# Layer 1 of a two-layer encoder: v's two parts in one stationary, 384-wide weights split in pairs, last kept units in dead buffers

## The chip, the cores and the metric

The kernel runs on one core of a Trainium2 chip. The metric is the device time of one launch in microseconds (us); the time shown for a kernel is the median of its runs. Engines are named as in the profile: PE (TensorE matmuls), PEld (its weight loads), DVE (VectorE), ACT (ScalarE), POOL (GpSimd), SP (SyncE, here only a DMA queue). Each engine runs its own instructions in the order in which they were written to it; between engines there are semaphores.

## The reference

Two layers over x of 256 tokens by 1024 channels, all in float32. Each layer is a mixer and a channel sublayer:

```python
h = rms_norm(x, n1); proj = h @ w_in_l              # 1024 -> 2560
# 4 neighbourhood heads (a), 6 dilated heads (d), 6 grouped-query heads (c) on 2 key/value heads
out_a = neighbourhood_attention(...)                # softmax(q k^T * scale + bias) v
out_d = dilated_window_attention(...)
out_c = gqa_block_attention(...)
mix = concat([rms_norm(out_a, og_a), rms_norm(out_d, og_d), rms_norm(out_c, og_c)])
x = x + mix @ w_out_l
h = rms_norm(x, n2); g, u = split(h @ w_gate_up)    # 2 x 2816
x = x + (gelu(depthwise_conv(g)) * u) @ w_dn
```

Head size is 64, so two heads make 128 columns of the mixer's output.

## The kernel before

**Two parts.** Every float32 operand of a large product is split into a high part in TensorE's rounded float32 and a low part, the rest: `hi = round(z)` by ACT (a CAST in the profile, or an ACTIVATE with a scale) and `lo = z - hi` by DVE. A product is then three matmuls, hi·hi + hi·lo + lo·hi (`mm3`). Weights go by units of at most 2048 columns: `load` starts the DMA of a unit into one of four `raw` buffers from SP's queue, `split` makes its `wp_hi` and `wp_lo` (two buffers of each), in chunks: whole rows of 512 or 1024 columns, and single rows of 384 for the 384-wide projections (in a unit of four rows, four chunks).

**Kept units.** The six w_out units of layer 1 are split ahead, while layer 0's channel sublayer runs (`keep`), and stored to DRAM. In layer 1 `split` fetches them back with two DMAs each from POOL's queue into the same `wp_hi` and `wp_lo` buffers. They are, in the order of use, two for the dilated heads, two for the grouped-query heads (both 3 x 512 columns), two for the neighbourhood heads (2 x 512).

**Attention.** For each head: scores into a PSUM bank, softmax (`softens`: DVE adds the bias and finds the maximum, ACT takes exp with its sum, DVE the reciprocal, ACT scales), four transposes on PE (`turn`), the transposed probabilities split into `pT` hi (`act_ch`, ACT) and lo (`act_cl`, DVE), and the product with v (`weigh`). v is the stationary operand: 64 columns of the head beside 64 columns of zeros (`beside_zeros`), so that an even head fills rows 0 to 63 of the output bank `op` and an odd head adds rows 64 to 127. Three matmuls for each half of the keys, 256 columns each: six a head, twelve a pair. When a pair of heads is done, `mixed` scales the bank with the output norm's gain into `mixT_hi` (ACT) and `mixT_lo` (DVE) and squares it (`sqm`, ACT; POOL adds the squares of a group). After a group's last pair `group_rstd` turns the squares on PE, DVE sums them and POOL makes the root; then the group's out-projection is added to x with that root (`const_x<-psa_a`, DVE).

**End of the mixer.** The out-projections of the dilated and grouped-query groups and the later projections are PE's filler between the steps of attention. When the last group's root is there, x is complete by halves, x is transposed (`const_ident,const_x`) and made into `hT`, and the first gate product of the channel sublayer starts.

**What sets the order.** The program is recorded as a list of operations; a planner with fixed costs then gives every engine its order and every tile its slot. `PLACES` shifts single operations in rank before that. Nearly all instructions bear one helper's line in the profile, so groups are told apart by their tiles: `psa_a` and `psw_w` are the PSUM banks (four each), `act_s2k` are five working buffers of 512 columns that softmax uses, `const_v` the value tiles.

Of the kernel before, what the change touches and what calls it, by code (L numbers as in the profile page):

```python
# [23 lines left out]
HD = 64  # L24
# [14 lines left out]
NS2K = 5  # L39

# [184 lines left out]
def handover(a, b):  # L225
# [292 lines left out]
def encoder_kernel(  # L518
# [70 lines left out]
    with nc.later(1000):  # L589
# [8 lines left out]
        [const.tile([P, NT, 2 * n + 1, HD], F32R, tag=f"v{n}{i}", name=f"v{n}{i}") for i in range(2)]  # L598
# [45 lines left out]
    def load(i):  # L644
        v = views[i]
        if i in kept:
            raws.append(None)
            return
        a, b = v.shape[1], v.shape[2]
# [20 lines left out]
    def split(i):  # L670
# [3 lines left out]
        raw = raws[i]  # L674
        hi = wp.tile([P, UNIT], F32R, tag="hi", name=f"hi{i}", bufs=PARTS)
        lo = wp.tile([P, UNIT], F32R, tag="lo", name=f"lo{i}", bufs=PARTS)
        h = b if i < 2 else b * max(1, CHUNK // b)
# [201 lines left out]
    for l in range(DEPTH):  # L879
# [171 lines left out]
        def values_of(tiles, ps, c0, t, nh):  # L1051
            src = ps[:, c0 : c0 + nh * HD].rearrange("p (h d) -> p h d", d=HD)
            values([z[:, t, 1 : 2 * nh : 2] for z in tiles], src, t)

        def beside_zeros(tiles, h, odd):

            i = 2 * h + 1 - odd
            return [z[:, :, i : i + 2].rearrange("p t m d -> p t (m d)") for z in tiles]


        class Head:
# [49 lines left out]
            def weigh(self, op, first, last):  # L1111

                hi, lo = self.pT
                for kt in range(NT):
# [5 lines left out]
        def mixed(op, gi, i):  # L1120
# [4 lines left out]
            h = mixT_hi[:, k]  # L1125
            nc.scalar.activation(h, op, AF.Copy, scale=g)
# [124 lines left out]
        def weigh(i):  # L1251
            gi, h = groups[i]
            if h % 2 == 0:
                hold["op"] = psw.tile([P, S], F32, tag="w", name=f"o_{l}{i}")
# [287 lines left out]
```

## Time and profile before

| | us |
|---|---|
| median of three runs | 610.36 (610.24 to 610.68) |
| profiled execution, its own time | 611.12 |
| its span, first to last instruction | 609.3 |
| layer 0: mixer, channel sublayer | 0 to 118, 118 to 295 |
| layer 1: mixer, channel sublayer | about 304 to 420, 420 to 605 |

The boundaries of the stages are read from the windows and the timeline of PE. A row of the timeline gives the start, the length, the engine, the output tile and the operands, and in brackets the idle time before it with what ended it. Matmuls overlap in the pipeline, so what one costs on PE is the distance between two starts, not its length.

### The profile page before, as it was taken

To read this page: it belongs to the slowest core of one execution; us is meant where nothing else is said; L and a number is where in the kernel's file an instruction comes from. 1 tells how busy PE (TensorE), PEld (TensorE's weight loads), DVE (VectorE), ACT (ScalarE), POOL (GpSimd) and SP (SyncE) were. 2 spreads that over 40 slices of the span, in tenths; PEclk is the share of its full clock that TensorE was granted. 3 is DMA by queue.
4 is the path that set the end of the run, shared out by engine and by line. 5 is a ranking of instruction groups with operands and counts; after the bars stand their busy time and mean duration, and the time that the engine had idled before them with its cause. 6 is when DMAs were issued, how large, how long until landed. Compare 5 with 4: busy or idle time off the path is not lost.

```text
span 609.3 us, 9892 instructions
## 1 busy us (share of the span) xinstructions
PE 600.6 (99%) x3496; PEld 525.2 (86%) x3496; DVE 484.9 (80%) x989; ACT 428.4 (70%) x1065; POOL 84.6 (14%) x136
## 2 busy tenths in 40 slices
PE   8999999999999999999999999999999999999997
PEld 6999898888888888888899989887888888888886
DVE  4899987998779886978788898758977777777775
ACT  6889999686657666766598898757765556665661
POOL 2733130202400000000032214232000000000000
PEclk9999999999999999999999999999999999999999
DMA  8994223656598996999445626554666556556501
GB/s 272 296 294 143 62 79 107 208 175 240 185 219 288 318 338 220 373 311 305 142 142 189 224 70 242 184 199 139 208 207 200 169 185 208 173 176 204 198 10 69
DMA packets 85217, 121.44 MB, mean 199 GB/s; under 512 B 9880, under 2 KB 69880, under 8 KB 85168
## 3 DMA queue, kind: packets, MB, share of 16 engines
q1 hardware_dynamic: 82896, 112.17, 56.8%
q0 software_dynamic: 1728, 8.39, 4.0%
q8 instruction: 27, 0.44, 0.3%
q10 hardware_dynamic: 544, 0.26, 0.2%
q14 instruction: 22, 0.18, 0.1%
HBM read 110.93 MB, written 9.88 MB: 198 GB/s over the span
## 4 chain that ended last, share of the span: by engine, by line
PE 91%; POOL 2%; issue 2%; DMA 2%; ACT 1%; DVE 1%; SPq 0%; DVEq 0%; POOLq 0%
PE psw_w L472 50%; PE psa_a L472 41%; DMA wp_hi<-dram_khi 1%; POOL small_rstd L472 1%; DMA wp_raw<-in_w_in_dram 1%; ACT act_s2k L472 1%; POOL small_ms L472 0%; DVE const_x L472 0%; ACT act_hT L472 0%; POOL act_sck L472 0%; POOL act_scq L472 0%; ACT wp_hi L472 0%; SPq L472 0%; POOL const_gq L472 0%; POOL act_sqm L472 0%
## 5 line engine op out<-in xcount | busy, mean ns | idle before, releaser
L472 DVE TENSOR_TENSOR wp_lo<-wp_raw,wp_hi 128x512 fp32r<-128x512 f32 (+2 forms) x332 | 232.3, 734 | 55.1 <-ACT wp_hi L472 34.9
L472 ACT CAST wp_hi<-wp_raw 128x512 fp32r<-128x512 f32 (+2 forms) x332 | 202.4, 663 | 25.1 <-PE psw_w L472 9.9
L472 PE MATMUL psw_w<-act_hT,wp_hi 128*128 128x512 f32 x704 | 180.7, 393 | 0.0
L472 PEld LDWEIGHTS psw_w<-act_hT,wp_hi 128*128 128x128 f32 x704 | 127.8, 189 | 24.2
L472 PE MATMUL psa_a<-wp_hi,act_hT 128*128 128x384 f32 (+2 forms) x448 | 113.3, 333 | 2.0 <-ACT act_hT L472 1.3
L472 PEld LDWEIGHTS psw_w<-act_hT,wp_lo 128*128 128x128 f32 x704 | 98.4, 190 | 7.1
L472 PE MATMUL psw_w<-act_hT,wp_lo 128*128 128x256 f32 x704 | 103.0, 282 | 0.0
L472 PEld LDWEIGHTS psa_a<-wp_hi,act_hT 128*128 128x128 f32 x448 | 77.9, 189 | 5.0 <-ACT act_hT L472 1.6
L472 ACT COPY act_s2k<-psw_w 128x256 f32<-128x256 f32 x88 | 32.4, 373 | 61.7 <-PE psw_w L472 61.4
L472 PE MATMUL psa_a<-wp_lo,act_hT 128*128 128x384 f32 (+2 forms) x224 | 74.0, 332 | 0.1
L472 PE MATMUL psa_a<-wp_hi,act_cl 128*128 128x512 f32 (+1 forms) x176 | 68.8, 393 | 0.0
L472 PE MATMUL psa_a<-wp_lo,act_ch 128*128 128x512 f32 (+1 forms) x176 | 68.7, 392 | 0.0
L472 PE MATMUL psa_a<-wp_hi,act_ch 128*128 128x512 f32 (+1 forms) x176 | 68.3, 392 | 0.0
L472 DVE TENSOR_TENSOR act_s2k<-psw_w,act_s2k 128x256 f32<-128x256 f32 x88 | 36.6, 421 | 16.2 <-ACT act_s2k L472 15.9
L472 PEld LDWEIGHTS psa_a<-wp_lo,act_hT 128*128 128x128 f32 x224 | 42.2, 188 | 2.1 <-DVE wp_lo L472 1.0
L472 PEld LDWEIGHTS psa_a<-wp_hi,act_cl 128*128 128x128 f32 x176 | 33.1, 188 | 7.4
L472 PEld LDWEIGHTS psa_a<-wp_hi,act_ch 128*128 128x128 f32 x176 | 33.2, 189 | 6.7
L472 PEld LDWEIGHTS psa_a<-wp_lo,act_ch 128*128 128x128 f32 x176 | 33.1, 188 | 6.8
L472 DVE SCALAR_TENSOR_TENSOR act_s2k<-act_s2k,act_cw,act_s2k 128x255 f32<-128x255 f32 x88 | 36.8, 477 | 1.4 <-ACT act_s2k L472 1.3
L472 ACT ACTIVATE act_s2k<-act_s2k 128x512 f32<-128x512 f32 x22 | 13.9, 632 | 29.6 <-DVE act_s2k L472 29.6
L472 ACT ACTIVATE act_s2k<-act_s2k,act_cw 128x256 f32<-128x256 f32 x44 | 24.1, 595 | 15.0 <-DVE act_s2k L472 15.0
L472 POOL TENSOR_TENSOR small_rstd<-small_ms,const_mh 128x6 f32<-128x6 f32 (+2 forms) x26 | 31.3, 1204 | 2.1
(120 smaller groups left out, 795.2 us busy)
## 6 DMA issues: line engine op xcount, KB each, us to landing
wp_raw<-in_w_gate_up_dram SPq DMA_DIRECT2D x44, 1024.0 KB, 5.2
wp_raw<-in_w_down_dram SPq DMA_DIRECT2D x22, 1024.0 KB, 4.9
wp_raw<-in_w_in_dram SPq DMA_DIRECT2D x14, 768.0 KB, 4.7
wp_raw<-in_w_in_dram SPq DMA_DIRECT2D x8, 1024.0 KB, 8.9
wp_raw<-in_w_out_dram SPq DMA_DIRECT2D x8, 768.0 KB, 10.0
dram_khi<-act_mixT_hi SPq DMA_DIRECT2D x4, 768.0 KB, 4.4
dram_klo<-act_mixT_lo SPq DMA_DIRECT2D x4, 768.0 KB, 11.2
wp_lo<-dram_klo POOLq DMA_DIRECT2D x4, 768.0 KB, 4.7
```

Source lines behind the costliest of these rows:

```text
L472: getattr(o.engine.real, o.method)(*map(real, o.args), **{k: real(v) for k, v in o.kw.items()})
```

## The change

Five edits; the first two only for layer 1 (`ONE_BANK`).

1. The value tile holds the high and the low part of a head side by side, 128 columns, in place of the head and zeros: for the own-value heads the order is hi, lo, lo, hi for a pair, for the two key/value heads hi, lo, hi. ACT writes the high parts (twice for the key/value heads), DVE the low ones, for the own-value heads in two instructions in place of one.
2. `weigh` is two matmuls for each half of the keys, [hi|lo] by `pT` hi and [hi|lo] by `pT` lo: four a head, eight a pair. Each head of a pair has its own half of the bank. The two parts now lie in different partitions and have to be added: in `mixed` ACT copies the whole bank (128 x 512) to an `act_s2k` buffer, and DVE adds the other half's partitions of the copy to the bank, once for each head (64 x 256), into a new tile `mxm`. Gain, low part and squares are then taken from `mxm` and not from the bank.
3. The 384-wide units are split in chunks of two rows (768 columns).
4. The last two kept units (2 x 512 columns, for the neighbourhood heads) are fetched into the buffers `qc` and `kc` of the grouped-query heads' q and k, and this in `load`, not in `split`; they take no `wp_hi` and `wp_lo`.
5. Another `PLACES` table, with 75 entries for 58.

```diff
+ONE_BANK = (1,)
 PLACES = {
-    539: 34, 543: 38, 665: 15, 834: 24, 881: 160, 919: 134, 926: 7, 974: -38, 1092: 342, 1180: -15, 1181: -15,
...
+    315: 312, 320: 312, 462: 45, 522: -239, 523: -239, 526: -239, 527: -239, 540: -41, 587: 150, 654: -267, 894: 42,
...
     def load(i):
         v = views[i]
+        a, b = v.shape[1], v.shape[2]
+        n = a * b
         if i in kept:
             raws.append(None)
+            if 2 * n <= UNIT:
+                zs = [act.tile([P, n], F32R, tag=f"{'qk'[i % 2]}c{j}", name=f"kept{i}{j}", bufs=1) for j in range(2)]
+                for z, d in zip(zs, kept[i]):
+                    nc.gpsimd.dma_start(z, d)
+                raws[-1] = [z.rearrange("p (a b) -> p a b", b=b) for z in zs]
             return
...
-        h = b if i < 2 else b * max(1, CHUNK // b)
+        h = b if i < 2 else b * max(2 if b == _WD else 1, CHUNK // b)
...
             def weigh(self, op, first, last):
                 hi, lo = self.pT
+                if l in ONE_BANK:
+                    for kt in range(NT):
+                        for i, z in enumerate(self.pT):
+                            nc.tensor.matmul(
+                                op[:, self.h % 2], self.v[0][:, kt], z[:, kt],
+                                start=kt == 0 and i == 0, stop=kt == NT - 1 and i == 1,
+                            )
+                    return
...
             h = mixT_hi[:, k]
+            if l in ONE_BANK:
+                whole = act.tile([P, S], F32, tag="mxm", name=f"mxm{gi}{l}{i}", bufs=2)
+                small_ = act.tile([P, NT, S], F32, tag="s2k", name=f"mxs{gi}{l}{i}", bufs=NS2K)
+                nc.scalar.copy(small_, op)
+                for e, (mine, other) in enumerate(((LOW, HIGH), (HIGH, LOW))):
+                    nc.vector.tensor_tensor(whole[mine], op[mine, e], small_[other, e], op=ALU.add)
+                op = whole
             nc.scalar.activation(h, op, AF.Copy, scale=g)
             nc.vector.scalar_tensor_tensor(mixT_lo[:, k], op, g, h.bitcast(F32), ALU.mult, ALU.subtract)
```

The order moves on all engines. Three places matter below. The first is PE at the end of attention in layer 1, from the last pair's second head on. `const_v600` is the own-value tile's high part (in the change the tile with both parts), `const_v610` its low part, `act_ch`/`act_cl` are the split probabilities, `psa_a<-wp_..,act_mixT` an out-projection of a group, `act_sqm` the squares to be turned for the last group's root. Before:

```order
L472 MATMUL psw_w0_83<-act_ch0_774,const_v600_91 128x256
L472 MATMUL psw_w0_83<-act_cl0_791,const_v600_91 128x256
L472 MATMUL psw_w0_83<-act_ch0_774,const_v610_101 128x256
L472 MATMUL psa_a2_302<-wp_lo0_149,act_mixT_hi0_856 128x512
...
L472 MATMUL psw_w2_124<-const_ident0_89,act_sqm1_967 128x128 x2
...
L472 MATMUL psa_a0_157<-wp_hi1_240,act_mixT_lo0_916 128x512
L472 MATMUL psw_w1_117<-const_ident0_89,const_x0_79 128x128 x4
L472 MATMUL psw_w0_83<-const_ident0_89,const_x0_79 128x128 x4
L472 MATMUL psa_a2_302<-wp_hi0_141,act_mixT_hi0_856 128x512
```

And in the change, where the last two units are read from `act_kc` and `act_qc`:

```order
L477 MATMUL psw_w1_117<-act_ch0_747,const_v600_91 128x256
L477 MATMUL psw_w1_117<-act_cl0_758,const_v600_91 128x256
L477 MATMUL psa_a3_326<-wp_hi0_141,act_mixT_lo0_878 128x512
...
L477 MATMUL psa_a1_175<-act_kc00_910,act_mixT_hi0_832 128x512
...
L477 MATMUL psw_w3_166<-const_ident0_89,act_sqm1_939 128x128 x2
...
L477 MATMUL psa_a3_326<-act_qc10_752,act_mixT_hi0_832 128x512
L477 MATMUL psw_w2_124<-const_ident0_89,const_x0_79 128x128
L477 MATMUL psw_w1_117<-const_ident0_89,const_x0_79 128x128
...
L477 MATMUL psa_a0_157<-act_qc00_741,act_mixT_lo0_878 128x512
L477 MATMUL psw_w3_166<-act_hT0_146,wp_hi0_141 128x512
```

Between the last `const_v` product and the first `const_x` transpose there are 21 out-projection products of 512 columns before and 29 in the change; behind the transposes there were twelve more (a whole unit), now five, split around them.

The second place is ACT at the same point: it makes the last `act_ch`, and then serves the last two pairs. Before:

```order
L472 CAST act_ch0_774<-psw_w3_166 128x512
L472 ACTIVATE act_mixT_hi0_856<-psw_w1_117,const_gains0_122 128x256
L472 ACTIVATE act_sqm1_967<-psw_w1_117 128x256
L472 ACTIVATE act_mixT_hi0_856<-psw_w0_83,const_gains0_122 128x256
L472 ACTIVATE act_sqm0_866<-psw_w0_83 128x256
```

In the change:

```order
L477 CAST act_ch0_747<-psw_w0_83 128x512
L477 COPY act_s2k3_197<-psw_w2_124 128x512
L477 ACTIVATE act_sqm1_939<-act_mxm0_3717 128x256
L477 COPY act_s2k4_223<-psw_w1_117 128x512
L477 ACTIVATE act_mixT_hi0_832<-act_mxm0_3717,const_gains0_122 128x256
L477 ACTIVATE act_mixT_hi0_832<-act_mxm1_3763,const_gains0_122 128x256
L477 ACTIVATE act_sqm0_840<-act_mxm1_3763 128x256
```

Two copies of a bank are added, and the last pair's copy stands behind the squares of the pair before it.

The third place is POOL, where it fetches the kept units: the third unit (`wp_hi_240`, `wp_lo_248`, DRAM tiles `khi`/`klo`) was next after the first group's root, and it now stands behind the four loads of the last two units. Before:

```order
L472 TENSOR_TENSOR small_rstd_460<-small_ms_454,const_mh_85 128x2 [waits Pool_49]
L472 DMA wp_lo_248<-dram_klo_2446 128x1536 [waits DMAHW5_49,DMASW0_49,PE_49]
L472 TENSOR_TENSOR act_sqm_866<-act_sqm_866,act_sqm_967 128x256 [waits Activation_49]
L472 DMA wp_hi_240<-dram_khi_2431 128x1536 [waits DMAHW3_49,DMASW1_49,PE_49]
L472 DMA wp_lo_149<-dram_klo_2618 128x1536 [waits DMAHW3_49,DMASW2_49,PE_49]
```

In the change:

```order
L477 TENSOR_TENSOR small_rstd_465<-small_ms_459,const_mh_85 128x2 [waits Pool_49]
L477 DMA act_kc_910<-dram_khi_2694 128x1024 [waits DMAHW7_49,PE_49]
L477 DMA act_kc_916<-dram_klo_2714 128x1024 [waits DMAHW1_49]
L477 DMA act_qc_741<-dram_khi_2819 128x1024 [waits DMAHW5_49]
L477 DMA act_qc_752<-dram_klo_2835 128x1024 [waits DMAHW7_49]
L477 DMA wp_hi_240<-dram_khi_2406 128x1536 [waits DMASW1_49,DMAHW3_49,DMASW0_49,PE_49]
L477 DMA wp_lo_248<-dram_klo_2421 128x1536
```

More of the change, by code (lines that the diff above doesn't have):

```diff
@@ L597, in encoder_kernel @@
     vown, vkv = (
-        [const.tile([P, NT, 2 * n + 1, HD], F32R, tag=f"v{n}{i}", name=f"v{n}{i}") for i in range(2)]
+        [const.tile([P, NT, max(2 * n + 1, 6), HD], F32R, tag=f"v{n}{i}", name=f"v{n}{i}") for i in range(2)]
         for n in (H_DIL, H_GKV)
@@ L674, in split @@
         raw = raws[i]
+        if isinstance(raw, list):
+            parts.append(raw)
+            return
         hi = wp.tile([P, UNIT], F32R, tag="hi", name=f"hi{i}", bufs=PARTS)
         lo = wp.tile([P, UNIT], F32R, tag="lo", name=f"lo{i}", bufs=PARTS)
-        h = b if i < 2 else b * max(1, CHUNK // b)
+        h = b if i < 2 else b * max(2 if b == _WD else 1, CHUNK // b)
         if i in kept:
@@ L1055, in beside_zeros @@
         def beside_zeros(tiles, h, odd):
+            if l in ONE_BANK:
+                i = 3 * h + odd if len(tiles[0].shape) and tiles is vkv else 2 * h
+                return [tiles[0][:, :, i : i + 2].rearrange("p t m d -> p t (m d)")]
             i = 2 * h + 1 - odd
```

26 lines of the change are left out of this document (24 added, 2 removed), and 12 rows, old and new, of the table PLACES.

## The prediction

> **What bounds the kernel now.** I read the page first: engine totals and the chain of waits.
>
> ```profile
> span 609.3 us, 9892 instructions
> PE 600.6 (99%) x3496; PEld 525.2 (86%) x3496; DVE 484.9 (80%) x989; ACT 428.4 (70%) x1065; POOL 84.6 (14%) x136
> PE 91%; POOL 2%; issue 2%; DMA 2%; ACT 1%; DVE 1%; SPq 0%; DVEq 0%; POOLq 0%
> ```
>
> PE is busy almost throughout and holds 91% of the chain, so work taken from PE counts nearly in full if PE does not then wait. But a busy share is a mean over stages, so the windows come next: layer 1's mixer, its channel sublayer, and two stretches of attention.
>
> ```profile
> core 0: us, PE busy (x) PEld busy (x) DVE busy (x) ACT busy (x) POOL busy (x), PEclk, DMA share, GB/s
> 295.00:420.00 125.00, 123.57 (x802) 111.36 (x801) 97.41 (x248) 98.63 (x320) 31.37 (x47) 1.00 0.51 171
> 420.00:605.00 185.00, 185.00 (x990) 159.02 (x988) 139.83 (x237) 110.95 (x203) 1.26 (x3) 1.00 0.51 168
> 350.00:370.00 20.00, 20.00 (x142) 16.98 (x140) 19.67 (x60) 18.86 (x56) 2.67 (x5) 1.00 0.33 106
> 370.00:420.00 50.00, 48.60 (x325) 42.37 (x325) 34.77 (x83) 35.07 (x102) 16.40 (x26) 1.00 0.55 191
> ```
>
> In the channel sublayer PE never waits: it starts when the mixer ends and lasts as long as before. So the change is decided in the mixer, where PE has 1.4 us of idle time and DVE and ACT are near 80% (97.41 and 98.63 of 125). From 350 to 370, softmax of the dilated heads beside the grouped-query preparation, DVE is full: 19.67 of 20; behind it 15 of its 50 us are free. The two waits of PE that its timeline shows in this mixer:
>
> ```profile
> 397.66 0.47 PE L472 MATMUL psa_a<-wp_hi,act_mixT_lo 128*128 128x512 f32 x1
> 398.39 0.50 PE L472 MATMUL psa_a<-wp_hi,act_mixT_hi 128*128 128x512 f32 x1 [0.26 <-DMA wp_hi<-dram_khi]
> 414.42 0.40 PE L472 MATMUL psa_a<-wp_hi,act_mixT_lo 128*128 128x512 f32 x1
> 415.92 1.09 PE L472 MATMUL psw_w<-const_ident,const_x 128*128 128x128 f32 x8 [1.10 <-DVE const_x L472]
> ...
> 419.18 0.40 PE L472 MATMUL psa_a<-wp_lo,act_mixT_hi 128*128 128x512 f32 x1
> 419.42 0.39 PE L472 MATMUL psa_a<-wp_hi,act_mixT_lo 128*128 128x512 f32 x1
> ```
>
> A 512-column product takes 0.232 us from start to start (the last two rows), so the first wait is 0.73 - 0.23 = 0.50 us, for the third kept unit's DMA, and the second 1.50 - 0.23 = 1.27 us, for the last additions to x.
>
> **The change part by part.** First the products with v.
>
> ```profile
> 304.00:420.00 116.00, 15.33 (x96) 13.42 (x96) 2.86 (x6) 2.91 (x6) 0.00 (x0) 1.00 0.52 173
> 408.85 0.28 PE L472 MATMUL psw_w<-act_cl,const_v 128*128 128x256 f32 x1
> 408.96 0.40 PE L472 MATMUL psw_w<-act_ch,const_v 128*128 128x256 f32 x2
> 409.20 0.28 PE L472 MATMUL psw_w<-act_cl,const_v 128*128 128x256 f32 x1
> 409.32 0.28 PE L472 MATMUL psw_w<-act_ch,const_v 128*128 128x256 f32 x1
> 409.44 0.39 PE L472 MATMUL psa_a<-wp_lo,act_mixT_hi 128*128 128x512 f32 x1
> ```
>
> The first row is the windows view of the value tiles alone: 96 products in layer 1. Two for three leaves 64. Five of them go from 408.85 to 409.44, so one costs 0.118 us. PE loses 32 x 0.118 = **3.78 us**. The same shape and width stay, so nothing suggests another pace.
>
> What it adds is the fold: for each of eight pairs a copy of a bank on ACT and two additions on DVE.
>
> ```profile
> L472 ACT CAST act_ch<-psw_w 128x512 fp32r<-128x512 f32 x32 | 19.1, 598 | 5.0 <-PE psw_w L472 2.9 <-DVE small_ss L472 1.9
> L472 DVE TENSOR_TENSOR act_s2k<-psw_w,act_s2k 128x256 f32<-128x256 f32 x88 | 36.6, 421 | 16.2 <-ACT act_s2k L472 15.9
> 382.20 0.74 DVE L472 TENSOR_TENSOR act_ko<-psw_w,act_ko 128x256 fp32r<-128x256 f32 x2
> L472 DVE TENSOR_TENSOR wp_lo<-wp_raw,wp_hi 128x1024 fp32r<-128x1024 f32 x44 | 54.1, 1234 | 24.7 <-PE psw_w L472 16.9 <-ACT wp_hi L472 7.7
> L472 DVE TENSOR_TENSOR wp_lo<-wp_raw,wp_hi 128x384 fp32r<-128x384 f32 x64 | 33.1, 555 | 5.7 <-ACT wp_hi L472 5.6
> ```
>
> A copy takes 0.60 us, an addition of 256 columns 0.42 alone and 0.33 behind another (two in 0.74). The trace has no addition on 64 partitions whose operands lie in different halves; a row's time follows its columns, not its partitions, so I take 0.33, with 0.42 above and nothing below, since 256 columns have to pass. That is 8 x 0.60 = 4.8 us on ACT and 16 x 0.33 = 5.3 us on DVE, spread from about 355 to the end of the mixer. It lies beside PE's filler, except where DVE is full and behind the last pair. The low parts of v in two instructions add four fixed costs of some 0.1 us, in the same place.
>
> [...]
>
> Chunks of 768: 14 units lose two instructions each on ACT and on DVE. Midway between 512 columns (0.687, in the rows on 128x512) and 1024, 768 cost DVE about 0.96 for twice 0.555, so DVE gains at most 14 x 2 x 0.15 = 4.2 us and ACT about the same, but where PE does not wait for either. Counted as 0; against it, the first chunk is ready some 0.7 us later (0.4 on DVE, 0.3 on ACT); PE covers that with the unit before, over 2 us of products, and without the cover it would cost 0.7 at one or two places. Range -0.3 to +1.
>
> ```profile
> L472 DVE TENSOR_TENSOR wp_lo<-wp_raw,wp_hi 128x512 fp32r<-128x512 f32 x224 | 145.2, 687 | 24.8 <-ACT wp_hi L472 21.5 <-PE psw_w L472 3.0
> ```
>
> **The end of the mixer.** Before, the chain from the last pair ran like this (first row the last gain on ACT):
>
> ```profile
> 409.64 0.47 ACT L472 ACTIVATE act_mixT_hi<-psw_w,const_gains 128x256 fp32r<-128x256 f32 x1 [2.96 <-PE psw_w L472]
> 412.82 0.41 DVE L472 TENSOR_REDUCE small_ss<-psw_w 128x2 f32<-128x256 f32 x1
> 413.61 0.71 POOL L472 TENSOR_TENSOR small_rstd<-small_ms,const_mh 128x2 f32<-128x2 f32 x1
> 414.45 1.41 DVE L472 SCALAR_TENSOR_TENSOR const_x<-psa_a,small_rstd,const_x 128x512 f32<-128x512 f32 x2 [1.06 <-PE psa_a L472]
> L472 DVE SCALAR_TENSOR_TENSOR act_hT<-psw_w,const_gains,act_hT 128x256 fp32r<-128x256 f32 x32 | 13.9, 478 | 3.2 <-ACT act_hT L472 3.2
> ```
>
> From 409.60 (the last product's end) to the transposes at 415.92 it is 6.3 us. The fold puts into it a copy (0.60), the additions (0.33 + 0.42) and, by ACT's order, the squares of the pair before, ahead of that copy (0.40): 8.05. In the new order the first transposes need x of one token half only, one addition of 0.7 less: 7.35. PE's filler up to there was 21 products, 21 x 0.232 = 4.9 us; now it is 29, 6.7 us, and with the small transposes 7.0, because the last two units no longer wait for `wp` buffers. So the wait of 1.27 shrinks to about 0.4. What is late next is the first gate product: it needs `hT` hi and lo (0.48 each, the last row for the low part) behind the transposes, and DVE has an addition to x and a chunk of `wp_lo` queued ahead of the low part, 2.2 us in all, where PE has three products and some transposes left, 1.2 to 1.4 us. That is some 0.8 us; before, twelve products covered it. Sum for the end: -1.27 + 0.4 + 0.8 = **-0.1**, between -1.3 (all covered) and +1.3 (twice that).
>
> **Softmax of the neighbourhood heads.** With a third less to do for v, PE reaches their transposes and products earlier, while ACT and DVE have two more folds there. Laying 0.35 for a bias (the two rows below), 0.7 for an addition to x and 0.69 for `act_cl` in DVE's new order, the low part of head 11 is ready 0.55 us after PE is through with the rows ahead of its product; at head 13 another 0.2. I take **+0.6**, from 0 to 1.5.
>
> ```profile
> 392.32 0.42 DVE L472 CUSTOM_DVE_ANT_0 act_s2k<-psw_w,act_nab 128x256 f32<-128x256 f32 x1
> 392.67 0.42 DVE L472 CUSTOM_DVE_ANT_0 act_s2k<-psw_w,act_nab 128x256 f32<-128x256 f32 x1
> L472 DVE TENSOR_TENSOR act_cl<-psw_w,act_ch 128x512 fp32r<-128x512 f32 x32 | 21.7, 687 | 4.5 <-ACT act_ch L472 4.1
> ```
>
> **The kept units.**
>
> ```profile
> 390.19 0.60 POOL L472 DMA_DIRECT2D wp_lo<-dram_klo  x1 [5.12 <-PE psa_a L472]
> 391.50 0.57 POOL L472 DMA_DIRECT2D wp_hi<-dram_khi  x1
> GB/s 0 0 0 160 209 344 455 418 406 418 418 270 49 0 0 0 0 0 0 0 16 0 25 172 258 356 504 234 197 184 233 295 315 182 204 115 11 0 135 233
> 390.97 1.70 PE L472 MATMUL psw_w<-act_ko,act_qo 64*128 64x256 f32 x24
> 393.16 0.60 PE L472 MATMUL psw_w<-const_ident,act_s2k 128*128 128x128 f32 x4
> ```
>
> The four loads of the last two units (2.1 MB) now go out as soon as the last grouped-query scores free `kc`, and the third unit (1.57 MB) stands behind them in POOL's order: four issues of 0.58 and their data. Between those scores and the first product with the third unit PE has 26 products of 512, 13 of 256, 24 of scores and 12 transposes, 6.0 + 1.5 + 1.7 + 1.2 = 10.4 us. POOL starts about 0.5 after the scores. The row of GB/s is the DMA view from 380 to 400 in slices of 0.5 us: the second kept unit's two loads take ten slices, 1.57 MB in some 4.6 us, 0.34 MB/us with a middle of 0.41. First data come 1.5 us after an issue (POOL's issue of that unit starts at 380.17). At 0.34 to 0.40 the high part (2.9 MB) lands 9.2 to 10.5 us after the scores, and the low part up to 0.8 us after PE wants it. I take +0.4 for this and -0.50 for the old wait: **-0.1**, between -0.5 and +5.5 (below).
>
> **Sum:** -3.78 - 0.1 + 0.6 - 0.1 = -3.4 us. Against the profiled execution, 611.12, that is 607.7; this lay 0.76 over the median, so the median goes from 610.36 to **607.0**. Layer 0 has no term: its PE order moves only through the chunks and the table.
>
> **The rivals.**
>
> 1. *All waits go.* If filler covers the end and DMA is in time: -3.78 - 1.27 - 0.50 = -5.5, 604.8. For it: the eight added filler products (1.9 us) exceed the fold's length. Against: the first gate product loses its cover. Chance 0.15.
> 2. *DVE becomes the bound while it is full.* The dilated pairs' three folds (3 x 0.66 = 2.0) and the split low parts (0.4) come behind a DVE that is busy 19.67 of 20 us. If PE's projections run out first, up to 2.4 us come back: 609.4. Against: PE did not wait at all in that stretch (20.00 of 20), and DVE can catch up in its 15 free us behind it. Chance 0.13. [...]
> 3. *Slower: the third kept unit comes late.* Its two loads took fifteen slices in the same row, from 391 to 398.4, when PE got its operand, alone in the queue; its high part alone 6.9 us from its issue at 391.50. At 1.57 MB in 6.9 us, 0.23 MB/us, the 2.9 MB ahead and of the high part land 14.5 us after the scores, 4.1 after PE wants them, and the low part costs another 1.9: +6 in place of -0.1, 612.9. It decides from a delay of 4.7 us on. Against: the unit before it flowed at 0.34. Chance 0.08.
> 4. *The saving is not made*, because the new order only moves PE's waits about: 610.4. PE's idle time in the mixer is too small for that now. Chance 0.06.
>
> **How the numbers follow.** The forecast has 0.58, with its own range 605.8 to 608.3. A measurement of this kernel tells 0.2%, 1.2 us, from no change: faster is below 609.1. Faster: 0.58 + 0.15 + half of rival 2 = 0.79. Within 0.2%: the other half and rival 4, 0.12. Slower: rival 3 and a little of 4, 0.09. The range reaches to rival 1 and to rival 2's end, 604.7 to 609.7, and leaves out rivals 3 and 4.
>
> **What would show it.** Right: 64 value products in layer 1 at 0.118 us; a channel sublayer of layer 1 that starts some 3.4 us earlier after the mixer's start and lasts as long. Fold additions of 0.33 to 0.42; waits under 1 us before the third kept unit and at the first gate product. Wrong: a wait of PE of some us on `wp_hi<-dram_khi` (rival 3), waits on `act_cl` or `wp_lo` between 345 and 370 (rival 2), fold additions far above 0.42, or new waits in layer 0.

## The result, and the profile after

| | before | after |
|---|---|---|
| median of 21 runs each, us | 610.36 (609.68 to 611.78) | 611.49 (610.53 to 612.27) |
| ratio, 95% interval | 1 | 1.0016 (1.001 to 1.0023) |
| span of the profiled execution | 609.3 | 609.8 |

The forecast was 607.0 with a range to 609.7. The change saves nothing; the time lies 1.1 us above before, just inside the 0.2% taken as no change. The page after: engine totals and the chain of waits.

```profile
span 609.8 us, 9790 instructions
PE 600.4 (98%) x3464; PEld 522.7 (86%) x3464; DVE 489.3 (80%) x981; ACT 429.0 (70%) x1045; POOL 87.6 (14%) x136
PE 89%; DVE 4%; ACT 3%; POOL 2%; issue 1%; DVEq 0%; POOLq 0%; ACTq 0%
```

PE has 32 instructions fewer, and the span is not shorter. The chain now runs for 4% over DVE, where it was 1%. The windows of the stages, columns as before the change, and at the end that of the value tiles alone:

```profile
295.00:420.00 125.00, 122.51 (x776) 108.78 (x774) 104.97 (x253) 103.42 (x317) 33.52 (x47) 1.00 0.53 175
425.00:605.00 180.00, 180.00 (x959) 154.63 (x959) 135.78 (x230) 106.41 (x191) 0.00 (x0) 1.00 0.51 172
350.00:370.00 20.00, 20.00 (x139) 17.18 (x138) 19.09 (x64) 19.23 (x55) 3.27 (x6) 1.00 0.29 93
370.00:420.00 50.00, 47.51 (x306) 39.38 (x302) 42.31 (x100) 41.37 (x116) 17.90 (x26) 1.00 0.56 196
304.00:420.00 116.00, 12.04 (x64) 9.96 (x64) 3.51 (x10) 3.28 (x6) 0.00 (x0) 1.00 0.53 178
```

The mixer's DVE went from 97.41 to 104.97 us in the first window, and from 34.77 to 42.31 in the last 50 us. PE is idle 2.5 us in its last 50, where it was idle 1.4. The channel sublayer is full still: 180.00 of 180.

To see where time is lost I cut the span at three products of PE: the first scores of layer 0, the first projection product of layer 1, the first gate product of layer 1. Stretch A lies between the first two, B between the last two. Before:

```profile
45.77 1.70 PE L472 MATMUL psw_w<-act_ko,act_qo 64*128 64x256 f32 x24
...
307.37 0.52 PE L472 MATMUL psa_a<-wp_hi,act_hT 128*128 128x384 f32 x2
...
419.65 0.40 PE L472 MATMUL psw_w<-act_hT,wp_hi 128*128 128x512 f32 x1
```

After, with PE's waits in between:

```profile
45.59 1.70 PE L477 MATMUL psw_w<-act_ko,act_qo 64*128 64x256 f32 x24
...
52.11 0.28 PE L477 MATMUL psa_a<-wp_lo,act_hT 128*128 128x256 f32 x1
53.23 0.33 PE L477 MATMUL psw_w<-const_ident,act_s2k 128*128 128x128 f32 x1 [0.84 <-ACT act_s2k L477]
...
308.35 0.34 PE L477 MATMUL psa_a<-wp_hi,act_hT 128*128 128x384 f32 x1
...
371.61 0.28 PE L477 MATMUL psa_a<-wp_lo,act_hT 128*128 128x256 f32 x1
373.05 0.66 PE L477 MATMUL psw_w<-const_ident,act_s2k 128*128 128x128 f32 x4 [1.16 <-ACT act_s2k L477]
...
398.68 0.39 PE L477 MATMUL psw_w<-act_cl,const_v 128*128 128x256 f32 x1 [0.20 <-DVE act_cl L477]
...
417.20 0.44 PE L477 MATMUL psw_w<-const_ident,const_x 128*128 128x128 f32 x2 [0.53 <-DVE const_x L477]
...
420.11 0.50 PE L477 MATMUL psw_w<-act_hT,wp_hi 128*128 128x512 f32 x1 [0.65 <-DVE act_hT L477]
```

A is 261.60 before and 262.76 after: +1.16, where no term was. B is 112.28 and 111.76: -0.52, where some -3.4 was expected. (In the change two more of the transposes of x lie inside B, 0.2 us, so for like work A lost 1.4 and layer 1's mixer gained 0.7.) The rows answer for B as follows, each wait from start to start less the product between:

| layer 1's mixer, us | forecast | PE's rows |
|---|---|---|
| products with v | -3.78 | -3.78 (32 x 0.118) |
| wait at 371, behind the dilated heads' fold | 0 (rival 2) | +1.32 |
| end: transposes of x, first gate product | -0.1 | 0.68 + 0.82 - 1.27 = +0.2 |
| wait for the third kept unit gone, head 11 | -0.50 + 0.4 + 0.6 | 0.38 - 0.50 = -0.1 |
| scores, at 385 and 394 | 0 | +0.7 |
| the rest, about a dozen steps of 0.1 to 0.2 each | 0 | +0.9 |

The last line is what is left of the gain of 0.7. The profile alone thus names layer 0, DVE behind the fold, and the scores; the runs below take them one by one. What the products themselves cost came out as said, 0.23 for the two from the first row's start to the next's, with one on `act_cl` between:

```profile
397.08 0.28 PE L477 MATMUL psw_w<-act_ch,const_v 128*128 128x256 f32 x1
...
397.31 0.28 PE L477 MATMUL psw_w<-act_ch,const_v 128*128 128x256 f32 x1
```

### The profile page after: what moved, and what is told of

Its sections match the earlier page's. It is cut to its first block, busy times and chain, and to the rows that moved or that the text cites. A ratio compares the mean times of both kernels' runs of the same rounds, so it can differ in the third digit from the quotient of the medians.

```text
span 609.8 us, 9790 instructions
## 1 busy us (share of the span) xinstructions
PE 600.4 (98%) x3464; PEld 522.7 (86%) x3464; DVE 489.3 (80%) x981; ACT 429.0 (70%) x1045; POOL 87.6 (14%) x136
## 4 chain that ended last, share of the span: by engine, by line
PE 89%; DVE 4%; ACT 3%; POOL 2%; issue 1%; DVEq 0%; POOLq 0%; ACTq 0%
PE psw_w L477 51%; PE psa_a L477 38%; ACT act_s2k L477 2%; DVE const_x L477 1%; POOL small_rstd L477 1%; DVE wp_lo L477 1%; POOL small_ms L477 1%; ACT wp_hi L477 0%; DVE act_mxm L477 0%; DVE act_z L477 0%; DVE act_cl L477 0%; ACT act_z L477 0%; DVE act_mixT_lo L477 0%; ACT act_ch L477 0%; ACT act_hT L477 0%
## 5 line engine op out<-in xcount | busy, mean ns | idle before, releaser
L477 DVE TENSOR_TENSOR wp_lo<-wp_raw,wp_hi 128x512 fp32r<-128x512 f32 (+3 forms) x304 | 229.3, 785 | 62.8 <-ACT wp_hi L477 38.9
L477 ACT CAST wp_hi<-wp_raw 128x512 fp32r<-128x512 f32 (+3 forms) x304 | 199.7, 705 | 19.8 <-PE psw_w L477 9.4
L477 ACT COPY act_s2k<-psw_w 128x256 f32<-128x256 f32 (+1 forms) x96 | 37.2, 391 | 67.6 <-PE psw_w L477 67.5
L477 PE MATMUL psa_a<-wp_hi,act_ch 128*128 128x512 f32 x176 | 68.3, 392 | 0.0
L477 POOL TENSOR_TENSOR small_rstd<-small_ms,const_mh 128x6 f32<-128x6 f32 (+2 forms) x26 | 29.9, 1151 | 2.1
```

The lines of the kernel that those rows point to most:

```text
L477: getattr(o.engine.real, o.method)(*map(real, o.args), **{k: real(v) for k, v in o.kw.items()})
```

## The experiments

All runs in one table; A and B are from each run's profiled execution, the ratio from its timed rounds against before. Where there is no ratio, the kernel was executed once. Executions of one kernel differ by up to 2.1 us (before: 609.68 to 611.78), so these four runs are read by A and B, not by their times. B repeats well: with the same layer 1 it is 111.76, 111.84 and 111.78 in after, e1 and e3. A is 261.26 to 261.36 in the five runs with layer 0 as before, but 262.76 to 263.24 in the six with the changed layer 0 as it is (after, e2, e5, e7, e9, e10).

| run | what is edited | A | B | median us | ratio (95%) |
|---|---|---|---|---|---|
| before | | 261.60 | 112.28 | 610.36 | 1 |
| after | | 262.76 | 111.76 | 611.49 | 1.0016 (1.001 to 1.0023) |
| e1 | layer 0: bias loads first | 262.22 | 111.84 | 611.0 | 1.0008 (0.9999 to 1.0017) |
| e2 | fold on one column | 262.81 | 109.76 | 609.78 | 0.998 (0.9971 to 0.9989) |
| e3 | layer 0 as before | 261.32 | 111.78 | 610.09 | 0.9992 (0.9984 to 1.0001) |
| e4 | e1 and e2 | 262.54 | 109.59 | 609.43 | 0.9975 (0.9964 to 0.9985) |
| e5 | scores paired | 263.00 | 111.69 | 611.42 | 1.0015 (1.0007 to 1.0024) |
| e6 | e3 and e5 | 261.33 | 111.69 | 609.86 | 0.9994 (0.9985 to 1.0002) |
| e7 | additions in one half | 263.12 | 111.37 | 611.19 | one execution |
| e8 | POOL's squares on one column | 261.87 | 111.24 | 610.06 | one execution |
| e9 | only the additions on one column | 263.24 | 109.76 | 610.57 | one execution |
| e10 | weight chunks behind x | 262.77 | 111.96 | 611.79 | one execution |
| e11 | e6 in a newly planned order | 263.26 | 111.46 | 611.51 | 1.0009 (1.0 to 1.0018) |
| e12 | e6, squares moved on POOL | 261.30 | 111.69 | 610.03 | 0.9991 (0.9982 to 0.9999) |
| e13 | e6, last two pairs unfolded | 261.26 | 114.17 | 612.95 | 1.0046 (1.003 to 1.0062) |
| e14 | e12 and e13 | 261.36 | 113.57 | 612.09 | 1.0038 (1.0025 to 1.005) |

### Layer 0: e1 and e3

SP issues the weight loads in one queue, and in layer 0 also a store of the neighbourhood bias to DRAM (`dram_scr`) and the two loads that read it back. Before:

```profile
26.58 0.36 SPq L472 DMA_DIRECT2D dram_scr<-act_nab  x1
28.82 0.38 SPq L472 DMA_DIRECT2D wp_raw<-in_w_in_dram  x1
30.07 3.40 SPq L472 DMA_DIRECT2D act_nab<-dram_scr  x2
```

After, with DVE's additions to that bias:

```profile
28.19 0.37 SPq L477 DMA_DIRECT2D wp_raw<-in_w_in_dram  x1
28.65 0.52 SPq L477 DMA_DIRECT2D dram_scr<-act_nab  x1
33.42 0.39 SPq L477 DMA_DIRECT2D wp_raw<-in_w_in_dram  x1
34.00 3.73 SPq L477 DMA_DIRECT2D act_nab<-dram_scr  x2
...
45.94 2.09 DVE L477 SCALAR_TENSOR_TENSOR act_nab<-act_nab,const_na 128x576 f32<-128x576 f32 x3 [2.03 <-DMA act_nab<-dram_scr]
```

One more weight load stands ahead of the bias: in the planner's new order one now comes before the store (28.19), and one stands between the store and the loads, as before. Whether the chunks of 768 or the table moved it there is not shown. The load at 28.19 waits for its `raw` buffer, and the store waits behind it, though POOL has written the bias by 27.10; before, the store went at 26.58, as soon as POOL was done. The bias loads go out 3.9 us later than before. DVE then stands 2.03 us in its fixed order, softmax is late, and PE waits at 52.1 (1.12 - 0.12 = 1.0 us).

e1 moves the load at 33.42 behind the two bias loads (the numbers are places in the recorded program):

```diff
+            order = self.order()
+            order.remove(370)
+            order.insert(order.index(395) + 1, 370)
```

> The changed kernel with one DMA moved: in layer 0 the weight load that stands in SP's queue ahead of the two loads of the neighbourhood bias (act_nab) goes behind them. Theory L (late bias): those two loads go out at 34.0 us in place of 30.1, DVE stands 2.03 us before its three additions to act_nab, the first softmax is late by that and PE waits 1.0 us at 52.2. Then DVE's 2.03 us go, the wait at 52.2 falls under 0.3 and the time from 611.5 to about 610.6. Theory C (the chunks of 768 or the table's order of DVE's other work cost layer 0 its 1.2 us): the wait stays, 611.3 to 611.7.

e3 takes edit 3 and the new table from layer 0 and leaves layer 1 as changed:

```diff
-        h = b if i < 2 else b * max(2 if b == _WD else 1, CHUNK // b)
+        h = b if i < 2 else b * max(2 if b == _WD and i >= PER_LAYER else 1, CHUNK // b)
```

> The changed kernel, but layer 0 as it was before: chunks of 384 in layer 0 and the old table's entries for it; layer 1 with the new table and the change. Theory L and theory C both expect layer 0's 1.2 us back: 610.3, with the x transposes of layer 0 at 117.9 us again. What lies between this run and the one with the bias loads moved is then the chunks' and the table's. If layer 0's loss comes from something that both layers share, 611.5.

In e1 SP and DVE show the step:

```profile
33.85 1.70 SPq L480 DMA_DIRECT2D act_nab<-dram_scr  x2
...
42.83 2.09 DVE L480 SCALAR_TENSOR_TENSOR act_nab<-act_nab,const_na 128x576 f32<-128x576 f32 x3
```

DVE's wait is gone, PE's fell to 0.42, and A is 0.54 shorter; the ratio fell by 0.0008, half a microsecond (the two intervals overlap, so it is the profile that carries this). The bias loads start no earlier, though, at 33.85: SP's waits in e1 show that it stood 5.0 us for the store to land, where it stood 0.8 before the change. What the edit shortened is their issue, 1.70 us for 3.73. e3 takes off the whole loss: A 261.32, B unchanged, and the ratio goes from 1.0016 to 0.9992, 1.5 us. So layer 0 costs 1.4 to 2.0 us of A, by the spread of the runs that keep its changed order, and the load between store and bias loads about a third of that: 262.22 and 262.54 in e1 and e4, against a mean of 262.95. The rest goes with the chunks or the table. The late store is the likeliest part of it, but no run moves the load ahead of the store, so this is not shown. PE's wait at 52 is unsteady: 0.35 to 1.48 us in the executions that keep the changed order there.

### The fold on DVE: e2, e4, e9, e7

DVE behind the second dilated pair, after; then POOL's addition beside it:

```profile
367.45 0.68 DVE L477 TENSOR_TENSOR act_cl<-psw_w,act_ch 128x512 fp32r<-128x512 f32 x1
368.17 0.86 DVE L477 TENSOR_TENSOR act_mxm<-psw_w,act_s2k 64x256 f32<-64x256 f32 x2
369.06 1.29 DVE L477 TENSOR_TENSOR wp_lo<-wp_raw,wp_hi 128x512 fp32r<-128x512 f32 x2
370.27 0.95 DVE L477 SCALAR_TENSOR_TENSOR act_mixT_lo<-act_mxm,const_gains,act_mixT_hi 128x256 fp32r<-128x256 f32 x1
371.25 1.89 DVE L477 TENSOR_REDUCE small_nm<-psw_w 128x2 f32<-128x512 f32 x3
...
369.97 0.97 POOL L477 TENSOR_TENSOR act_sqm<-act_sqm,act_sqm 128x256 f32<-128x256 f32 x1 [0.65 <-ACT act_sqm L477]
```

The additions, the low part and a chunk of weights stand ahead of the maxima (`small_nm`) of the next scores, whose transposes PE waits for at 371.61. Two additions take 0.89 us from their start to that of the next instruction, 0.44 each, and not 0.33. One of them is 0.42 long (mean of the 16), as an addition of 128x256 is; what is missing is the overlap, 0.09 between two of those in the trace before.

e2 keeps the program's order and lets the copy and both additions work on one column:

```diff
+        short = lambda v: v[(slice(None),) * (len(v.shape) - 1) + (slice(0, 1),)]
...
+                args = [short(v) if i in self.folds else v for v in o.args]
...
+                nc.folds |= set(range(len(nc.ops), len(nc.ops) + 3))
```

> The changed kernel with the same order of instructions, but the fold's copy and its two additions do one column of 256 (so the mixed values are not computed; two tiles are filled once at the start). Theory F (the fold's own time on ACT and DVE is what PE waits for in layer 1): the wait of 1.32 us at 371.7 falls under 0.4, that of 0.37 at 398 goes, and of the 0.68 + 0.82 at the mixer's end at least 0.7 goes, about -2.2 us: 609.3. Theory O (the new order itself, with the softmax placed later behind the work of the same engine, makes these waits): less than 0.4 us of it, 611.1 or more.

e4 is e1 and e2 together, e9 shortens the additions alone and leaves ACT's copy whole.

> The bias loads moved and the fold of one column, together (the mixed values of layer 1 are not computed). Theories L and F together, if they add up: 611.5 - 0.9 - 2.2 = 608.4. If only L holds 610.6, if only F 609.3. The prediction's 607.0 is reached in no case if some 0.8 us are lost to shorter runs of like products on PE.

> As the run with the fold of one column, but the fold's copy on ACT is whole and only its two additions on DVE do one column (the mixed values are not computed). If DVE's part is what PE waits for (6.8 us of DVE's time in layer 1 against 4.8 of ACT's), the wait at 371.7 falls to 0.5 as it did there and the mixer of layer 1, from its first x transposes to its first gate product, takes 111.9 us (113.8 in the changed kernel, 111.8 with the whole fold at one column). If ACT's copy is, it stays at 113.5.

PE in e2 at the place of the wait, then e9's window of the mixer:

```profile
372.33 0.65 PE L483 MATMUL psw_w<-const_ident,act_s2k 128*128 128x128 f32 x4 [0.34 <-ACT act_s2k L483]
```

```profile
295.00:420.00 125.00, 123.36 (x785) 110.39 (x785) 102.58 (x256) 104.72 (x319) 33.27 (x47) 1.00 0.53 179
```

e2 takes 2.00 us off B and its ratio to 0.998; the wait at 371 falls from 1.32 to 0.50. e4 takes a little more off A, 0.27. e9 has the same B as e2, 109.76, with ACT busier than in the change (104.72 to 103.42): so DVE's additions make up the 2.0 us, and ACT's copies cost little. The two runs don't wait in the same places, so the equal sums are partly chance: e9 has no wait at 371, where its low part also escaped POOL (next section), but 0.52 for the third kept unit at 403.7, which e2 doesn't have; both wait 0.54 at 397.

e7 takes the copy's operand from the same half of the partitions as the bank's, so that nothing switches halves within an addition:

```diff
-                    nc.vector.tensor_tensor(whole[mine], op[mine, e], small_[other, e], op=ALU.add)
+                    nc.vector.tensor_tensor(whole[mine], op[mine, e], small_[mine, e], op=ALU.add)
```

> The fold's second operand is taken from the same half of the partitions as the first (so the mixed values are not the right sum); nothing else differs. Theory H (an addition whose operands lie in another half than those of the instruction before starts only when that has finished): two additions in a row take 0.86 us from the start of the first to the end of the second in the changed kernel, 0.43 each from start to start; with one switch fewer inside each addition, but still one between the two, the gap between start and start stays near 0.43. Rival (it is the operands of one addition in two halves that cost): start to start falls to 0.33. Time within 0.5 us of the changed kernel in both.

```profile
367.35 0.68 DVE L477 TENSOR_TENSOR act_cl<-psw_w,act_ch 128x512 fp32r<-128x512 f32 x1
367.95 0.85 DVE L477 TENSOR_TENSOR act_mxm<-psw_w,act_s2k 64x256 f32<-64x256 f32 x2
368.83 1.29 DVE L477 TENSOR_TENSOR wp_lo<-wp_raw,wp_hi 128x512 fp32r<-128x512 f32 x2
```

From the start of `act_cl`, 0.68 long, to that of the first addition it is 0.60 in place of 0.72: with its operands in one half the addition starts 0.08 before `act_cl` ends, where it started 0.04 behind it. The two additions, which still lie in different halves, take as long as in the change from their start to that of the next instruction, 0.88 for both (0.89). So the step got shorter where the half no longer changes and stayed where it still does; no run has two of these additions in the same half. B is 0.39 shorter than in the change.

### POOL beside DVE: e8, e10, e12

The low part at 370.27 took 0.95 us; the same kind takes 0.47 to 0.48 in six of its seven other places after, and 0.67 in the seventh, at 394.47, where POOL's addition (394.12, 0.73) runs beside it too. At 370.27 it runs beside POOL's addition of squares, which is longer too. e8 shortens all of POOL's additions of squares, in both layers, to one column, so the group norms are not computed:

```diff
+                args = [v[:, :1] if i in self.squares else v for v in o.args]
```

> POOL's additions of the squares do one column of 256 in both layers (so the group norms are not computed). Theory P: the low part of the mixed values at 370.3 takes 0.95 us in place of 0.48 because POOL's addition (0.97 in place of 0.74) runs beside it; then it takes 0.48, the softmax behind it is 0.5 earlier and the wait of 1.32 at 371.7 falls to 0.85. Rival: the 0.95 stays, it has another cause, and the wait too.

```profile
369.26 0.47 DVE L479 SCALAR_TENSOR_TENSOR act_mixT_lo<-act_mxm,const_gains,act_mixT_hi 128x256 fp32r<-128x256 f32 x1
...
368.96 0.43 POOL L479 TENSOR_TENSOR act_sqm<-act_sqm,act_sqm 128x1 f32<-128x1 f32 x1 [0.64 <-ACT act_sqm L479]
```

The low part takes 0.47, and PE's wait at 371 falls from 1.32 to 0.84, as much as the low part got shorter; B falls by 0.52. (A is lower too, but POOL's first addition of squares is at 68.8 us, behind the wait at 52, which was 0.35 in this execution; how much of A is the edit's can't be told.) What the two contend for, no run shows. In e9 the low part came first, at 370.28, and took 0.48; POOL's addition came at 370.36 and took 0.99. So too after the change at 402.24: 0.48 for the low part, 0.92 for the addition at 402.40. And before the change, where the low part read the bank in PSUM, both ran side by side at full pace:

```profile
365.89 0.48 DVE L472 SCALAR_TENSOR_TENSOR act_mixT_lo<-psw_w,const_gains,act_mixT_hi 128x256 fp32r<-128x256 f32 x1
365.94 0.74 POOL L472 TENSOR_TENSOR act_sqm<-act_sqm,act_sqm 128x256 f32<-128x256 f32 x1 [8.52 <-DVE act_cl L472]
```

So this meeting is a cost of the fold too: its new tile `mxm` lies in SBUF, and the low part is now taken from there.

At the end of the mixer the same meeting shows on a tiny instruction of POOL, the mean for the last root:

```profile
414.23 1.28 DVE L477 TENSOR_TENSOR wp_lo<-wp_raw,wp_hi 128x512 fp32r<-128x512 f32 x2
...
414.25 1.32 POOL L477 TENSOR_SCALAR small_ms<-small_ss 128x2 f32<-128x2 f32 x1 [1.65 <-DVE small_ss L477]
```

It starts with two chunks of weights on DVE and ends with them, and the additions to x wait for it. e10 puts these two chunks behind the additions to x:

```diff
+            for i in (4089, 4087):
+                order.remove(i)
+                order.insert(order.index(4068) + 1, i)
```

> The changed kernel with two instructions moved: the two chunks of wp_lo that DVE does at 414.2, beside POOL's small_ms, go behind the next two additions to x. Theory P (a DVE instruction with two SBUF inputs keeps POOL from its own): small_ms takes 0.2 us in place of 1.32, the additions to x start 1.1 earlier and the wait of 0.68 at the x transposes goes; the one of 0.82 at the first gate product stays or grows by up to 0.2, as the chunks now stand ahead of hT: -0.5 to -0.7. Rival (small_ms is long for another reason, such as its own semaphore): 1.32 stays and nothing changes.

```profile
414.28 0.19 POOL L481 TENSOR_SCALAR small_ms<-small_ss 128x2 f32<-128x2 f32 x1 [1.65 <-DVE small_ss L481]
...
416.55 0.38 PE L481 MATMUL psw_w<-const_ident,const_x 128*128 128x128 f32 x2
...
420.33 0.50 PE L481 MATMUL psw_w<-act_hT,wp_hi 128*128 128x512 f32 x1 [1.59 <-DVE act_hT L481]
```

The mean takes 0.19 in place of 1.32, and PE no longer waits for x. But the chunks now stand ahead of the low part of `hT`, and the wait at the gate product grows to 1.76: 0.68 and 0.82 went into one, and B is 0.2 longer. So in both of these orders it is DVE's work in sum that PE waits for at the mixer's end, in the one place or the other.

e12 tried on e6 to part the two at 370 by their order on POOL.

> Layer 0 as before and the scores in turn, and beside them POOL's addition of the squares that stood beside DVE's low part at 370 put behind the three row maxima that follow. Theory P (the two engines shut each other out): the low part takes 0.48 in place of 0.95, the wait of 1.3 before the transposes at 371 falls to 0.85, and the mixer of layer 1 from 113.7 to 113.2; time 609.4, ratio to the kernel before about 0.9985. Rival: the addition delays something else by as much, 609.9.

```profile
368.89 0.96 DVE L484 SCALAR_TENSOR_TENSOR act_mixT_lo<-act_mxm,const_gains,act_mixT_hi 128x256 fp32r<-128x256 f32 x1
```

Nothing that POOL now ran ahead of the addition held it back, so it met the low part all the same; B is e6's to the hundredth. The run decides nothing.

### The scores and the planned order: e5, e6, e11

In the change's order the products of one head's scores stand behind one another in two places, where before those of the two halves of the partitions took turns. The two bursts, after:

```profile
385.29 1.32 PE L477 MATMUL psw_w<-act_kc,act_qc 64*128 64x256 f32 x12
...
393.87 2.04 PE L477 MATMUL psw_w<-act_ko,act_qo 64*128 64x256 f32 x24
```

Before, the 12 took 0.98 and the 24 took 1.70. e5 puts the members of each burst together again in the order in which they were recorded, e6 adds that to e3:

```diff
+            for burst in self.bursts.values():
+                at = min(map(order.index, burst))
+                order = [i for i in order if i not in burst]
+                order[at:at] = burst
```

> The changed kernel with the score products of each pair of heads in turn again (one of the one head, one of the other, as before the change): the new table had put the products of one head behind those of the other in two bursts of layer 1. Theory S: two products of 64 rows in different halves of PE run side by side only when they alternate; in the trace 12 of them take 0.91 us in turn and 1.25 head after head. Then the bursts at 385 and 394 take 0.91 and 1.63 in place of 1.25 and 1.97, and the time falls by 0.7: 610.8. Rival: those bursts have slack behind them, softmax is no earlier, and PE waits for it instead: less than 0.2 us.

> Layer 0 as before (chunks of 384 there and the old table's entries for it) and the scores in turn, with the fold and all else of the change in layer 1. If the three losses found (layer 0 1.2 to 1.4, scores 0.7, fold 2.1) add up, what stays is the fold's: 611.5 - 1.4 - 0.7 = 609.4, some 1 us under the kernel before, ratio 0.998 to 0.999. If they overlap (PE then waits elsewhere), 610.0 to 610.3.

```profile
394.19 1.70 PE L482 MATMUL psw_w<-act_ko,act_qo 64*128 64x256 f32 x24
```

The products are as quick as before, but B is only 0.07 shorter, and e6's 0.09 shorter than e3's: PE waits for softmax a moment later instead, as at 397.96 for `act_ch` in e6. Nearly all of the 0.7 in the table above thus covered waits that would have come anyway.

e11 plans the order anew, with prices nearer to those measured: 0.106 us more for an addition on 64 partitions, products of scores cheap only where they take turns, 1.7 us for a bias load's issue.

> Layer 0 as before and the scores in turn, as in the run of those two; beside them the order of layer 1 made anew, with three prices in the planner set to what the traces show: an addition of the fold 0.44 us from start to start in place of 0.33, score products side by side only in turn, and the bias loads' issue of 1.7 us each. Theory O (the fold's work fits beside PE's if the order is made with its right price): of the 1.3 at 371, the 0.8 around 397 and the 0.7 + 0.8 at the mixer's end at least half goes, -1.8 us against the run with the old order: 608.0, ratio to the kernel before about 0.996. Theory F (ACT and DVE are too full for the fold in any order): 609.5 to 610, ratio 0.999.

B is 111.46, 0.2 below e6. So no better place for the fold was found there; this is one more order and no proof that none exists. The new prices moved layer 0's order too, against the intent of leaving it as before: at its heads behind 104 us PE waits twice, the first time 0.94 us for `act_ch` at 105.33, and A is 263.26. The kernel's total therefore says nothing on layer 1.

### Folding fewer pairs: e13, e14

e13 leaves the last group's two pairs as before, with zeros beside v and three products; e14 adds e12's edit.

```diff
-            if l in ONE_BANK:
+            if l in ONE_BANK and gi < 2:
```

> Layer 0 as before and the scores in turn; and the two pairs of the neighbourhood heads, the last of the mixer, weighed as before (three products, no fold; the zeros beside their values are written anew by POOL). PE does 8 products more (+0.94). Theory D (at the mixer's end DVE's queue is what PE waits for, 0.7 + 0.8, and the fold's four additions with their copies are 2.4 us of that chain): the two waits fall to 0.3 in all, and that of 0.3 to 0.5 at the last softmax goes: -1.6 + 0.9 = -0.6, time 609.2. Rival (other work fills DVE's queue there anyway): the waits stay and the time grows by 0.9, 610.7.

> The last two runs' edits together. If both theories hold and the gains add: 609.9 - 0.5 - 0.6 = 608.8, ratio to the kernel before about 0.9975, which would be faster than both kernels. If only one holds 609.3.

```profile
412.19 2.48 DVE L482 TENSOR_TENSOR wp_lo<-wp_raw,wp_hi 128x512 fp32r<-128x512 f32 x4
...
418.18 1.09 PE L482 MATMUL psw_w<-const_ident,const_x 128*128 128x128 f32 x8 [1.12 <-DVE const_x L482]
...
421.03 0.50 PE L482 MATMUL psw_w<-act_hT,wp_hi 128*128 128x512 f32 x1 [1.76 <-DVE act_hT L482]
```

Both are slower than before, by 2.8 and 2.3 us by their ratios. Part of this is the clock: in four of e13's eight executions and two of e14's five the granted clock was 0.994 to 0.997, in no execution of another kernel here below 0.998, and these took 613.02 to 615.82 us. At 0.999 or more e13 took 611.29 to 612.89 and e14 611.69 to 612.09. Why only these two lost clock is open. The profiles are at full clock: against e6, B of e13 is 2.5 us longer, 0.94 of it the eight products that come back. The planner filled the freed room on DVE with four chunks of weights, ahead of the additions to x, and both waits at the end became longer (1.29 and 1.97 us). What the fold of the last pairs alone is worth, these runs can't say: the order moved with it.

## Why the prediction was wrong, step by step

- **"Layer 0 has no term"** failed: +1.4 us (A for like work; e3 takes it off). The prediction looked at PE's order there and left out SP's, where one more weight load stands ahead of the bias. Moving one of two loads out of the way (e1) gave back about a third; the rest, of which the late store is the likeliest part, has no run of its own.
- **The fold at nothing, "beside PE's filler"** failed: 2.0 us (e2 against the change; e9). The size was off, 0.44 an addition for 0.33, and the cover more so: behind a DVE that was full to 19.67 of 20 us the additions, the split low parts and the meeting with POOL came out as a wait of 1.32. That meeting was in no term: 0.5 of that wait (e8). This is rival 2, which had 0.13, at its place, though not in its size: it puts 2.4 on the dilated heads, where PE's wait is 1.32 and the additions of all eight pairs are worth 2.0, and it has no term for the scores and the small steps. Its 609.4 and layer 0's 1.2 to 1.4 give 610.6 to 610.8, where 611.49 was measured. The argument against rival 2, that DVE has 15 free us from 370 on, did not hold: the maxima that PE needs stand in DVE's order behind the fold, and free time later is no use to them.
- **The rest of the loss in layer 1**: 0.7 for the scores out of turn, which no term had, though mending it gave 0.1 (e5). The steps of 0.1 to 0.2, 0.9 in all, have no run of their own; e9 suggests that a part goes with DVE's additions, since its B falls by 2.0 and its waits by 0.9 in all.
- **Softmax of the neighbourhood heads** (+0.6, head 11 0.55): right in place, 0.38 on `act_cl` at head 11; none at head 13.
- **The end of the mixer** (-0.1): the two waits were named and sized, 0.4 and 0.8 against 0.68 and 0.82. POOL's mean, 1.13 us longer than alone, was not foreseen, nor does it decide (e10).
- **The kept units** (-0.1): the wait of 0.50 is gone, and none of the +0.4 put beside it came, so this went better than said; rival 3 is off. It is not far away: in e9, with 2 us less of B, it returns at 0.5. (Rival 3's own sum is uneven: +6 in place of -0.1 is 613.1 and the +5.5 of the range 612.6, where 612.9 stands. Nothing hangs on it.)
- **Chunks of 768**: DVE's price was right, 0.966 for an estimated 0.96 (row below), and the range of +1 at the other end fell short of what they or the table set off in layer 0.
- **Products with v** (-3.78): 64 of them at 0.118, and the channel sublayer as long as before. Rivals 1 and 4: not all waits went, and the saving was made and given back.

The row of the 768-wide low parts, from the groups of instructions after (count, busy time, mean ns):

```profile
L477 DVE TENSOR_TENSOR wp_lo<-wp_raw,wp_hi 128x768 fp32r<-128x768 f32 x28 | 26.6, 966 | 6.6 <-ACT wp_hi L477 6.6
```

The versions with layer 0 as before (e3, e6, e12) lie 0.06 to 0.09% under the kernel before, less than can be told. e2 and e4, which leave the fold's sums out, lie 0.20 and 0.25% under it, with all or most of layer 0's loss still in them. No run leaves out both; by the ratios of e3 and e2, 1.5 and 2.2 us off 611.49 would leave 607.8, an estimate that takes it that the two add. By it the two steps that failed make up 3.7 of the 4.5 us by which the forecast missed, and the last 0.8 stays open. In the orders tried, two products for three are worth nothing here as long as VectorE pays for the fold.

## What to carry to other kernels

Work moved from a busy engine to one that is busy 80% on average cost something here, where its queue had no room ahead of the next result that was waited for (DVE: 19.67 of 20 us from 350 to 370 before, and PE's wait of 1.32 after): read the busy share of the stretch in which each new instruction lands, and what stands behind it there. An edit of chunks or order also moved transfers in a queue (the bias loads of layer 0 from 30.07 to 34.00); follow each queue in every layer, the untouched ones too, and look for a store or load that now stands behind a transfer that has to wait. And a wait that is mended by moving its cause came back behind it where the engine's work in sum set the time (B fell by 0.07 in e5 and rose by 0.20 in e10), so shorten the work before its order.

## What the runs showed of the hardware

- **POOL and DVE slowed each other where DVE read two SBUF tiles.** A 128x2 instruction of POOL took 1.32 us beside two DVE chunks and 0.19 without them (e10); a low part on DVE 0.95 beside POOL's addition and 0.47 with that cut to one column (e8). Where the low part started first, it took 0.48 and POOL's addition 0.99 (e9) or 0.92 (after, 402.40). A low part that read PSUM lost nothing beside the same addition (before: 0.48 and 0.74).
- **Additions in alternating halves of the partitions took longer on DVE.** One of 64x256 took 0.44 us from start to start where the halves alternate (after), one of 128x256 took 0.33 behind another (before); the step ahead of the first fell from 0.72 to 0.60 with operands in one half (e7).
- **Products on half the rows were quicker in turns.** 24 scores products on 64 rows took 1.70 us with the halves in turn (before, e6) and 2.04 with one head behind the other in part of them (after); 12 took 0.98 (before) and 1.32 (after).
- **The bias loads held SP's queue.** The two loads took SP 3.4 and 3.7 us to issue before and after, 2.5 in e3 with the order of before, and 1.70 in e1. The weight load right behind them took up to 3.66 (after), where most take 0.37 to 0.39. Why is not shown.
